# A third column pair computed by seven products, with the keys' rotation beside them, in a Trainium2 encoder block

## The chip, the cores and the metric

The kernel runs on one core of a Trainium2 chip. The metric is device time in microseconds (us) of one whole execution, the median of three. Engines are named as in the profile: PE (TensorE, matrix products) with PEld (its weight loads), DVE (VectorE), ACT (ScalarE), POOL (GpSimd) and SP (SyncE, which here only issues transfers). Each engine executes its own list of instructions in order; an instruction that waits for another engine or for a transfer (a DMA) holds back all that stand behind it in the same list.

## What is computed

One layer of an encoder, for two requests (512 and 256 positions, 768 rows in all, width 2048), with shared weights. Cut to what matters here:

```python
h = rmsnorm(x, ln_mix_g);  z = h @ w_in            # 2560 columns
zf = z[..., :1024]   # 8 Fourier groups of 128 channels
q  = z[..., 1024:2048] # 16 query heads of 64
k, v = z[..., 2048:2304], z[..., 2304:]   # 4 heads each
of = per group: Re(fft2(zf)) @ w_fourier[g]
q, k = apply_rope(q), apply_rope(k)      # x*cos + rot(x)*sin
s = q @ k.T * 64**-0.5, within +-128 positions
m = maximum(max(s), sink);  p = exp(s - m) / (sum exp(s - m) + exp(sink - m))
x = x + concat(rmsnorm(of), rmsnorm(p @ v)) @ w_out
x = x + relu(rmsnorm(x) @ w_up)**2 @ w_down;  return rmsnorm(x)
```

All of it is in 32-bit floats. The kernel splits each operand into a high and a low part (`wh`, `wl` for weights) and sums three products of parts, so one product of the reference is three matmuls. ACT makes a high part (a copy that rounds), DVE the low part (a subtraction).

## The kernel before

The columns of `w_in` are worked in blocks of 256. First come the values `v`. Then 8 Fourier blocks of 128 channels, that is two pairs of 256-column blocks, are computed by **seven products**: a 2x2 block scheme with seven block products (`a11`, `s1`, `s2`, `s3`, `a22`, `s4`, `a12`) in place of eight. A step is one half of one product for one column block pair: 28 steps (`NP7`), each with 24 matmuls of 128x384 (`product7`, L277). In step n the code adds the weights of step n+3 where the scheme wants a sum (`sum7`, DVE), makes their high part (`high7`, ACT) and the low part of step n+2 (`low7`, DVE), and takes the results of step n-1 out of PSUM (`out7`): a copy on ACT (L297) or an add on DVE (L294), then a store of `z` to DRAM. The order on SP, ACT and DVE in this stage is the order of the code ("manual schedule").

The rest of the columns (keys, 2048 on, and four query blocks) come as 20 **pieces** of 48 matmuls of 128x384 (L830), four pieces for one pair of column halves. The weights of piece p+2 are split while piece p runs (`piece_split`, L69 for `wh`, L70 for `wl`). Among the pieces the 8 Fourier groups are done, one per piece: `fold`, `stage1` (three blocks, whose results become `ah` on ACT and `al` on DVE) and `stage2` (18 matmuls of 128x256, L659), whose result `of` POOL squares and sums (L669, L670) and ACT stores to DRAM (`ofd`). After the eighth group come the rotations: POOL multiplies with the sines (`cross`, L715), DVE with the cosines and adds (`turned`, L722 and L724), ACT and DVE split the result (`parts`, L740 and L741) and ACT stores it. A table `after(piece, fn)` says in which half piece each of these is written; outside the last piece a scheduler in the compiler may place it differently. In the last piece the order on SP, ACT, DVE and POOL is the code's own again. Finally `load_of(0)` loads the first Fourier results back (`ofr`), which the output projection (`pm`, L1077) splits (`ofh` on ACT, `ofl` on DVE) and multiplies between the attention products (L876 `s`).

In attention, DVE adds the mask and takes the maximum of each row in one instruction (L891), a second instruction negates it (L896), and ACT applies the exponential (L906).

Of the kernel before, what the change touches and what calls it, by code (L numbers as in the profile page):

```python
# [40 lines left out]
def hybrid_encoder(ctx: ExitStack, tc: tile.TileContext, a: dict):  # L41
# [75 lines left out]
    kr_d = dpool.tile([4 * P, T], F32, tag="k", name="k")  # L117
    qr_d = [[dpool.tile([2 * P, T], F32, tag=f"q{c}{i}", name=f"q{c}{i}") for c in "hl"] for i in range(NKV)]
# [79 lines left out]
    with ExitStack() as ph:  # L198
        hp = ph.enter_context(tc.tile_pool(name="hp", bufs=1, reuse_waits="tile"))
        pp = ph.enter_context(tc.tile_pool(name="pp1", bufs=4, space=PSUM))  # L200
# [7 lines left out]
        NP7 = 4 * len(names7)  # L208
# [5 lines left out]
        def load7(n):  # L214
            if n >= NP7:
                return
            x, g, e = names7[n // 4], n // 2 % 2, n % 2
            blocks = blocks7.get(x, (x,))
            raw7[n] = []
            for i, x in enumerate(blocks):  # L220
# [6 lines left out]
                nc.sync.dma_start(raw[:], w_in[2 * g + c][:, k0 : k0 + 4, :])  # L227
                raw7[n].append(raw)

        def sum7(n):  # L230
            if n >= NP7:
                return
            s, ge = names7[n // 4], n % 4
            x = raw7[n][0]
            if s == "s1":
                kept7[ge] = hq["p"].tile([P, 4, 256], F32, tag="ws", name="ws", bufs=4)
# [28 lines left out]
        def product7(n):  # L265
            w, g, e = n // 4, n // 2 % 2, n % 2
            bank = bank7[names7[w]]
            opens = w == 0 or names7[w] in ("s1", "a12")
            wh, wl = w7.pop(n)
            if e == 0 and opens:  # L270
                for r in range(2):
                    ps7[bank, g, r] = pp.tile([P, 512], F32, **(dict(tag="f", bufs=4) if bank == "Y" and 2 * g + r < 4 else dict(tag="ps", bufs=4)), name="p7")
            x = xs[w % 2]
            for i in range(4):
                for r in range(2):
                    for q, (l, o) in enumerate(((wh, 0), (wh, 1), (wl, 0))):
                        nc.tensor.matmul(  # L277
                            ps7[bank, g, r][:, :HALF], l[:, i, r * P : (r + 1) * P], x[:, o, 4 * e + i, :],
# [4 lines left out]
        def out7(n):  # L283
            while put7:
                put7.pop(0)()
            if n < 0 or n % 2 == 0:
                return
            s, g = names7[n // 4], n // 2 % 2
            c, t, how = take7[s]
            for r in range(2):  # L290
                ps = ps7[bank7[s], g, r][:, :HALF]
                if how == 1:
                    z = c7.pop((c, t, g, r))
                    nc.vector.tensor_tensor(out=z[:], in0=ps, in1=z[:], op=ALU.add)  # L294
                else:
                    z = hq["p"].tile([P, HALF], F32, tag=f"z{c}{t}", name="z7", bufs=2 if how else 4)
                    nc.scalar.activation(z[:], ps, AF.Copy)  # L297
                if how == 0:
                    c7[c, t, g, r] = z
                else:  # L300
                    dst = zf_d[4 * g + 2 * c + r]
# [1555 lines left out]
```

## Time and profile before

| | |
|---|---|
| median of three executions | 2574.53 us (2574.41 to 2574.83) |
| profiled execution, its own time | 2575.42 us |
| span of its trace | 2573.6 us |
| PE busy | 2561.6 us, 100% of the span |
| DVE / ACT / POOL busy | 70% / 44% / 10% |
| granted TensorE clock | 0.999 of full speed |
| seven products | 42.16 to 158.60 us |
| pieces | 158.60 to 362.39 us |
| attention with half of the output projection | from 362.39 us |

A busy share is the time in which an engine executes; an idle engine matters only if another waits for it. The chain of waits goes back from the last instruction to what released each one, so it names the engine that set the time. The windows table gives the same busy times for a stretch. The time of a group of instructions is the mean of one instruction; in a dense row of matmuls their distance is what counts, since a matmul's own time overlaps with the next one's.

### The profile page before, as it was taken

How to read it: one execution, taken by the hardware profiler on the slowest of the kernel's cores; microseconds unless marked ns; L12 is line 12 of the kernel's file. 1: busy time of each engine (PE TensorE's matmuls, PEld its weight loads, DVE VectorE, ACT ScalarE, POOL GpSimd, SP SyncE). 2: the span in 40 equal slices, each digit the busy share in tenths (PEclk: the TensorE clock that was granted, in tenths of full speed). 3: DMA queues.
4: the chain of work that ended last, by engine and by line, in shares of the span. 5: the costliest groups of instructions: out<-in, count | busy, mean ns of one | idle time of the engine just before them, and what ended most of it. 6: DMA issues, size and time to landing. Idle time of an engine off the chain costs nothing.

```text
span 2573.6 us, 34809 instructions
## 1 busy us (share of the span) xinstructions
PE 2561.6 (100%) x13467; PEld 2345.1 (91%) x13467; DVE 1797.7 (70%) x2222; ACT 1122.4 (44%) x1621; POOL 246.3 (10%) x345
## 2 busy tenths in 40 slices
PE   9999999999999999999999999999999999999998
PEld 9999998888899999999999999988888888888887
DVE  8866467786565565556777777667766766777687
ACT  7645337683234333333445544433333333333335
POOL 0102322223201001100000000100000000000000
PEclk9999999999999999999999999999999999999999
DMA  8753567455655455456666666775543662555364
GB/s 303 230 184 126 168 194 209 137 163 190 227 180 176 153 174 173 164 184 239 218 230 230 214 217 211 262 290 176 176 155 118 217 229 84 175 185 159 101 210 152
DMA packets 259815, 487.84 MB, mean 190 GB/s; under 512 B 20602, under 2 KB 147328, under 8 KB 259392
## 3 DMA queue, kind: packets, MB, share of 16 engines
q1 hardware_dynamic: 188112, 321.77, 39.1%
q10 hardware_dynamic: 58512, 112.05, 11.5%
q0 software_dynamic: 13024, 51.79, 6.0%
q8 instruction: 106, 1.74, 0.3%
q14 instruction: 61, 0.50, 0.1%
HBM read 365.99 MB, written 119.54 MB: 189 GB/s over the span
## 4 chain that ended last, share of the span: by engine, by line
PE 97%; DVE 2%; DMA 1%; ACT 0%; issue 0%; SPq 0%; DVEq 0%; POOLq 0%; POOL 0%; ACTq 0%
PE pu L1224 36%; PE pd L1659 35%; PE pm L1077 9%; PE pz L830 6%; PE p L277 5%; PE pv L442 1%; PE o L955 1%; PE t L933 1%; PE s L876 1%; PE pe L659 0%; PE pa L638 0%; PE ptx L137 0%; DVE p L891 0%; DMA ofr<-ofd 0%; DVE ofl L1061 0%
## 5 line engine op out<-in xcount | busy, mean ns | idle before, releaser
L1224 PE MATMUL pu<-xf,wh 128*128 128x384 f32 x3072 | 780.2, 334 | 0.0
L1224 PEld LDWEIGHTS pu<-xf,wh 128*128 128x128 f32 x3072 | 554.1, 188 | 1.5 <-ACT o L1242 1.2
L1659 PE MATMUL pd<-wl,sh 128*128 128x512 f32 x1332 | 517.7, 389 | 0.0
L1659 PE MATMUL pd<-wh,sh 128*128 128x512 f32 x1332 | 517.7, 389 | 0.0
L1659 PE MATMUL pd<-wh,sl 128*128 128x512 f32 x1332 | 517.5, 389 | 0.0
L1224 PE MATMUL pu<-xf,wl 128*128 128x384 f32 x1536 | 513.2, 334 | 0.0
L1636 ACT ACTIVATE wh<-rd 128x1024 fp32r<-128x1024 f32 x200 | 202.4, 1054 | 522.2 <-PE pd L1659 414.2
L1646 DVE TENSOR_TENSOR wl<-rd,wh 128x1024 fp32r<-128x1024 f32 x200 | 236.1, 1221 | 226.3 <-ACT wh L1636 225.5
L1204 ACT ACTIVATE wh<-ur 128x1024 fp32r<-128x1024 f32 x160 | 170.1, 1063 | 382.5 <-PE pu L1224 208.0
L1659 PEld LDWEIGHTS pd<-wh,sh 128*128 128x128 f32 x1332 | 250.1, 188 | 51.8
L1659 PEld LDWEIGHTS pd<-wh,sl 128*128 128x128 f32 x1332 | 250.0, 188 | 51.9 <-DVE sl L1647 0.3
L1659 PEld LDWEIGHTS pd<-wl,sh 128*128 128x128 f32 x1332 | 250.1, 188 | 51.6
L1224 PEld LDWEIGHTS pu<-xf,wl 128*128 128x128 f32 x1536 | 288.3, 188 | 0.0
L1210 DVE TENSOR_TENSOR wl<-ur,wh 128x1024 fp32r<-128x1024 f32 x160 | 195.4, 1221 | 76.1 <-ACT wh L1204 76.1
L1245 DVE TENSOR_TENSOR o<-pu,o 128x768 f32<-128x768 f32 x160 | 152.8, 956 | 122.3 <-PE pu L1224 114.8
L1629 DVE TENSOR_TENSOR rd<-rd 128x1024 f32<-128x1024 f32 x112 | 131.7, 1217 | 0.0
L1224 PE MATMUL pu<-xs,wh 128*128 128x384 f32 x512 | 129.8, 334 | 0.0
L1204 ACT ACTIVATE wh<-sx 128x1024 fp32r<-128x1024 f32 x64 | 67.9, 1062 | 130.6 <-PE pu L1224 101.9
L277 PE MATMUL p<-xs,wh 128*128 128x384 f32 x448 | 113.9, 334 | 0.0
L1647 DVE TENSOR_TENSOR sl<-sr,sh 128x768 fp32r<-128x768 f32 x111 | 105.5, 951 | 0.0
L1210 DVE TENSOR_TENSOR wl<-sx,wh 128x1024 fp32r<-128x1024 f32 x64 | 78.2, 1222 | 23.8 <-ACT wh L1204 23.6
L1224 PEld LDWEIGHTS pu<-xs,wh 128*128 128x128 f32 x512 | 92.4, 188 | 0.0
(293 smaller groups left out, 3849.3 us busy)
## 6 DMA issues: line engine op xcount, KB each, us to landing
rd<-in_w_down SPq DMA_DIRECT2D x176, 512.0 KB, 5.2
ur<-in_w_up SPq DMA_DIRECT2D x128, 512.0 KB, 3.9
sr<-sd SPq DMA_DIRECT2D x95, 384.0 KB, 5.4
pd<-o ACTq DMA_DIRECT2D x60, 384.0 KB, 2.3
o<-pd POOLq DMA_DIRECT2D x60, 384.0 KB, 6.1
sd<-sm ACTq DMA_DIRECT2D x60, 384.0 KB, 2.7
raw<-in_w_in SPq DMA_DIRECT2D x39, 512.0 KB, 4.3
raw<-in_w_out SPq DMA_DIRECT2D x32, 512.0 KB, 4.5
```

The source lines that it names most:

```text
L277: nc.tensor.matmul(ps7[bank, g, r][:, :HALF], l[:, i, r * P : (r + 1) * P], x[:, o, 4 * e + i, :], start=(opens and e == 0 and i == 0 and ...
L830: nc.tensor.matmul(ps[c][s][:, :HALF], w[:, i, cs], whole[j // 2][s][o][:, 4 * (j % 2) + i, :], start=first and n == 0, stop=stop and n == 2,)
L1077: nc.tensor.matmul(ps, l(k), w[:, k % 2, :], start=(k == 0 and n == 0), stop=(k == 7 and n == 2))
L1204: nc.scalar.activation(wh[:], raw[:], AF.Copy)
L1210: nc.vector.tensor_tensor(out=wl[:], in0=raw[:], in1=f32(wh[:]), op=ALU.subtract)
L1224: nc.tensor.matmul(ps[:, t, :HALF], w[:, i, t * P : (t + 1) * P], xb[:, o, i, :], start=(s == first_of[bank] and i == 0 and n == 0), stop= ...
L1245: nc.vector.tensor_tensor(out=o, in0=src, in1=o, op=ALU.add)
L1629: add = lambda x, y, op: nc.vector.tensor_tensor(out=x[:], in0=x[:], in1=y[:], op=op)
L1636: nc.scalar.activation(wh[:], t[:], AF.Copy)
L1646: nc.vector.tensor_tensor(out=wl[:], in0=t[:], in1=f32(wh[:]), op=ALU.subtract)
L1647: nc.vector.tensor_tensor(out=sl[:], in0=sr[:], in1=f32(sh[:]), op=ALU.subtract)
L1659: nc.tensor.matmul(o, l[:, q, ts], w[:, ns], start=(j == j0 and (q, t) == (0, 0)), stop=(j == j1 and (q, t) == (1, 2)),)
```

## The change

A third pair of column blocks, the keys (block 8) and one quarter of the queries (block 6), joins the seven products: 42 steps instead of 28, and 12 pieces instead of 20. `a11`, `s2`, `s3` and `a22` accumulate in six PSUM banks; `s1`, `s4` and `a12` share two further banks, which the next group of columns reuses. In each step the result of the step before is taken out first, and the first half of a step's own result right behind its product. The product's loop over its two row halves is the outer one. The keys are rotated in steps 29 to 40, in buffers of that stage; the cosines and sines, multiplied with the norm factor, go to DRAM and come back for the queries. The Fourier groups are written half a piece or more earlier, the other rotations among them. In attention mask, sink and queries are negated, and a minimum takes the place of maximum and negation.

```diff
-        NP7 = 4 * len(names7)
+        cols7 = ((0, 1), (2, 3), (6, 8))
+        NS7 = 2 * len(cols7)
+        NP7 = NS7 * len(names7)
...
         def product7(n):
...
-            for i in range(4):
-                for r in range(2):
+            for r in range(2):
+                if e == 0 and opens:
+                    ps7[own, g, r] = pp.tile([P, 512], F32, tag="t" if own else "x", bufs=2 if own else 6, name="p7")
+                for i in range(4):
...
+        def k_tables():
+            for name, src in (("cos", a["c_cos"]), ("sin", a["c_sin"])):
+                kr[name] = spare7()[:].rearrange("p a b -> p (a b)")[:, :T]
+                nc.sync.dma_start(kr[name], src)
...
+        def k_scale():
+            for name in ("cos", "sin"):
+                nc.vector.tensor_tensor(out=kr[name], in0=kr[name], in1=rb[:], op=ALU.mult)
...
+            for s in range(3):
+                step(k_at, 33 + 2 * s, lambda s=s: k_cross(s))
+                step(k_at, 34 + 2 * s, lambda s=s: k_turn(s))
+                step(k_at, 35 + 2 * s, lambda s=s: k_parts(s, 35 + 2 * s))
+            step(k_at, 29, k_tables)
+            step(k_at, 32, k_loads)
+            step(k_at, 32, k_scale)
+            step(k_at, 33, k_keep)
             for n in range(NP7):
-                for fn in high_at.get(n, ()):
-                    fn()
+                out7(n - 1, 1)
                 sum7(n + 3)
                 high7(n + 3)
                 low7(n + 2)
+                product7(n)
+                out7(n, 0)
...
-                product7(n)
-                out7(n - 1)
...
-            out7(NP7 - 1)
-            out7(-1)
+            out7(NP7 - 1, 1)
+            stores7()
+        pctx.close()
...
-        for pair, t, ahead in ((0, 10.5, 10), (2, 11.5, None), (3, 15, None), (1, 16.5, 12)):
...
+        for pair, ts in ((1, (2, 4, 6)), (2, (7.5, 8, 8.5)), (3, (9, 9.5, 10))):
+            for s, t in enumerate(ts):
+                after(t, lambda pair=pair, s=s: cross(pair, s))
+                after(t + 0.5, lambda pair=pair, s=s: (turned(pair, s), parts(pair, s)))
...
-        after(18, lambda: load_of(0, [kt["kp"].tile([P, 4, P], F32, tag="zy", name="ofr", bufs=2) for _ in range(2)]))
-        n_in = 4 * len(cols)
+        after(10.5, lambda: load_of(0, [kt["kp"].tile([P, 4, P], F32, tag="zy", name="ofr", bufs=2) for _ in range(2)]))
+        n_in = 4 * (len(cols) - 2)
...
-                scalar=sink[:, 4 * g + h : 4 * g + h + 1], op0=ALU.add, op1=ALU.max, accum_out=mx[:, h : h + 1],
+                scalar=sink[:, 16 + 4 * g + h : 17 + 4 * g + h], op0=ALU.add, op1=ALU.min, accum_out=nm[:, h : h + 1],
...
-        nc.vector.tensor_scalar(out=st["nm"][:, hs], in0=mx[:, hs], scalar1=-1.0, scalar2=None, op0=ALU.mult)
```

Three places show what that does to the lists. The first is the seam from the seven products to the pieces, on ACT. `z7` is a result of the seven products on its way to DRAM, `wh` the high part of a piece's weights, `tabh` that of a Fourier table. Before:

```order
L69 ACTIVATE wh_1841<-raw_1836 128x1024
L302 DMA zf4_74<-z7_1264 128x384
L302 DMA zf5_75<-z7_1266 128x384
L72 ACTIVATE xf01_1613<-d7_1685,gall_256 128x384 x4
L69 ACTIVATE wh_1847<-raw_1838 128x1024
L302 DMA zf0_70<-z7_898 128x384
L302 DMA zf1_71<-z7_900 128x384
L69 ACTIVATE wh_1857<-raw_1845 128x1024
```

In the change:

```order
L327 DMA zs1_79<-z7_2146 128x384
L327 DMA zs1_79<-z7_2148 128x384
L69 ACTIVATE tabh_2373<-tab_2381 128x512
L69 ACTIVATE tabh_2373<-tab_2382 128x512
L69 ACTIVATE wh_2405<-raw_2385 128x1024
L69 ACTIVATE wh_2411<-raw_2389 128x1024
```

Before, `wh_1841`, the weights of piece 0, stands ahead of six of the last stores; in the change `wh_2405`, the weights of piece 0, stands behind the last store (`z7_2148`, the second half of step 41) and behind two table splits.

The second is DVE among the pieces. `zs_2805` is a query pair under rotation, `zy_3748` POOL's product for its last third, `of_2989` the result of Fourier group 2, and `al_2885` the low part that `stage2` of group 3 multiplies. In the change:

```order
L340 TENSOR_TENSOR zs_2805<-zs_2805,cosr_2394 128x2x256
L352 SCALAR_TENSOR_TENSOR zs_2805<-zs_2805,zh_3674 128x2x256
L782 TENSOR_SCALAR of_2989<-pz2_2970 128x256
L342 TENSOR_TENSOR zs_2805<-zs_2805,zy_3679 128x256 x2
L750 TENSOR_TENSOR ft_3002<-pa_2997,ft_3002 128x256
L352 SCALAR_TENSOR_TENSOR zs_2805<-zs_2805,zh_3743 128x2x256
L340 TENSOR_TENSOR zs_2805<-zs_2805,cosr_2394 128x2x256
L70 TENSOR_TENSOR al_2885<-ft_3002,ah_2884 128x256
L342 TENSOR_TENSOR zs_2805<-zs_2805,zy_3748 128x256
L709 TENSOR_TENSOR zf_3084<-zf_3084,rb_286 128x768
L70 TENSOR_TENSOR al_2885<-pa_3007,ah_2884 128x256
```

and on POOL, at the same place:

```order
L336 TENSOR_TENSOR zy_3679<-zs_2805,sinr_2396 128x256 x2
L787 TENSOR_TENSOR sq_2992<-of_2989 128x768
L788 TENSOR_TENSOR ssf_2375<-ssf_2375,sq_2992 128x768
L336 TENSOR_TENSOR zy_3748<-zs_2805,sinr_2396 128x256 x2
```

Before, no rotation stood among the `al` rows of a Fourier group; in the change the second L340 row, which waits for `zy_3748`, stands ahead of all of group 3's `al` rows, and `zy_3748` stands on POOL behind the squares of group 2.

The third is the start of attention, on DVE. `wl_3877` and `wl_3928` are low parts that follow the last piece's first half, `ofl0` is the low part of the first Fourier results. Before:

```order
L70 TENSOR_TENSOR wl_3844<-raw_3690,wh_3843 128x1024
L70 TENSOR_TENSOR wl_3877<-raw_3769,wh_3876 128x1024
L843 COPY zs_3873<-pz_3603 128x384
L843 COPY zs_3873<-pz_3604 128x384
L1061 TENSOR_TENSOR ofl0_3926<-ofr_3837,ofh0_3925 128x512
L1061 TENSOR_TENSOR ofl0_3926<-ofr_3838,ofh0_3925 128x512
```

In the change:

```order
L70 TENSOR_TENSOR wl_3928<-raw_3810,wh_3927 128x1024
L340 TENSOR_TENSOR zs_3424<-zs_3424,cosr_2394 128x2x256
L342 TENSOR_TENSOR zs_3424<-zs_3424,zy_3884 128x256 x2
L352 SCALAR_TENSOR_TENSOR zs_3424<-zs_3424,zh_3934 128x2x256
L939 COPY zs_3924<-pz_3552 128x384
L939 COPY zs_3924<-pz_3553 128x384
L1153 TENSOR_TENSOR ofl0_3988<-ofr_3944,ofh0_3987 128x512
L1153 TENSOR_TENSOR ofl0_3988<-ofr_3945,ofh0_3987 128x512
```

The last third of the next-to-last rotation (`zs_3424`) now stands behind `wl_3928`, and the buffer of its `zy_3884` is the one that `ofr_3944` takes (tag `zy`, two buffers). PE's list is the same at this place before and after: the last pieces' matmuls, one pair of `s`, then `pm` with `ofh0`.

## Rows read from the trace of the kernel before

**Rows 1.** The page's first part: busy us of each engine, share of span.

```profile
PE 2561.6 (100%) x13467; PEld 2345.1 (91%) x13467; DVE 1797.7 (70%) x2222; ACT 1122.4 (44%) x1621; POOL 246.3 (10%) x345
```

**Rows 2.** Windows table: length, then busy PE, PEld, DVE, ACT, POOL; clock, DMA.

```profile
42.00:100.00 58.00, 58.00 (x337) 58.00 (x336) 52.22 (x41) 36.40 (x48) 3.42 (x6) 1.00 0.63 210
...
158.00:260.00 102.00, 102.00 (x669) 102.00 (x668) 62.40 (x144) 46.41 (x124) 17.20 (x11) 1.00 0.44 139
```

**Rows 3.** PE's waits from 158 to 700 us: total, times, longest.

```profile
PE s L876 <- DVE mx L891: 0.8, 1, 0.8
```

**Rows 4.** DVE groups, 40 to 160 us: busy, mean ns, idle before.

```profile
L262 DVE TENSOR_TENSOR wl<-raw,wh 128x1024 fp32r<-128x1024 f32 x7 | 8.5, 1215 | 0.0
L308 DVE TENSOR_TENSOR xr<-xr,xr 128x1536 f32<-128x1536 f32 x5 | 8.7, 1747 | 0.0
L294 DVE TENSOR_TENSOR z<-p,z 128x384 f32<-128x384 f32 x11 | 5.6, 549 | 0.0
L73 DVE SCALAR_TENSOR_TENSOR xf<-d,gall,xf 128x384 fp32r<-128x384 f32 x8 | 4.4, 614 | 7.9 <-ACT xf L72 7.9
```

**Rows 5.** ACT's list at the seam: two issues of stores (start, us).

```profile
156.19 0.92 ACTq L302 DMA_DIRECT2D zf<-z  x2
```

**Rows 6.** ACT groups, 158 to 420 us.

```profile
L69 ACT ACTIVATE wh<-raw 128x1024 fp32r<-128x1024 f32 x26 | 27.5, 1056 | 26.3 <-PE pz L830 17.8 <-DMA raw<-in_w_in 4.1 <-DVE zs L741 2.7
...
L69 ACT ACTIVATE tabh<-tab 128x512 fp32r<-128x512 f32 x2 | 1.3, 634 | 4.7 <-DMA tab<-in_c_pos 4.7
...
L1060 ACT ACTIVATE ofh<-ofr 128x512 fp32r<-128x512 f32 x2 | 1.2, 632 | 0.0
```

**Rows 7.** DVE groups, 158 to 420 us.

```profile
L724 DVE TENSOR_TENSOR zs<-zs,zy 128x256 f32<-128x256 f32 x28 | 13.3, 510 | 0.1
L722 DVE TENSOR_TENSOR zs<-zs,cosr 128x512 f32<-128x512 f32 x14 | 12.2, 873 | 8.7 <-POOL zy L715 8.7
L741 DVE SCALAR_TENSOR_TENSOR zs<-zs,zh 128x512 fp32r<-128x512 f32 x11 | 8.4, 783 | 1.7 <-ACT zh L740 1.7
...
L591 DVE TENSOR_TENSOR zf<-zf,rb 128x768 f32<-128x768 f32 x8 | 7.6, 951 | 7.4 <-DMA zf<-zf 7.4
...
L896 DVE TENSOR_SCALAR nm<-mx 128x1 f32<-128x1 f32 x27 | 4.1, 154 | 0.9
...
L664 DVE TENSOR_SCALAR of<-pz 128x256 f32<-128x256 f32 x8 | 3.4, 422 | 18.6 <-PE pz L659 18.6
```

**Rows 8.** POOL groups, 158 to 420 us.

```profile
L715 POOL TENSOR_TENSOR zy<-zs,sinr 128x256 f32<-128x256 f32 x28 | 27.0, 991 | 51.6 <-ACT zs L843 21.5 <-DVE ofl L1061 18.2 <-DVE zs L724 9.9
L670 POOL TENSOR_TENSOR ssf<-ssf,sq 128x768 f32<-128x768 f32 x7 | 13.0, 1851 | 0.5
L669 POOL TENSOR_TENSOR sq<-of 128x768 f32<-128x768 f32 x7 | 10.3, 1468 | 67.2 <-DVE of L664 56.0 <-DMA zf<-zf 11.2
```

**Rows 9.** PE's list: last of one group's stage 2, first of the next one's.

```profile
205.32 0.28 PE L659 MATMUL pz<-tabh,al 128*128 128x256 f32 x1
...
216.10 0.28 PE L659 MATMUL pe<-tabh,ah 128*128 128x256 f32 x1
```

**Rows 10.** DVE's list between them: first and last of the next group's `al`.

```profile
208.98 0.91 DVE L70 TENSOR_TENSOR al<-ft,ah 128x256 fp32r<-128x256 f32 x1 [2.09 <-ACT ah L69]
...
215.17 0.28 DVE L70 TENSOR_TENSOR al<-pa,ah 1x128 fp32r<-1x128 f32 x1
```

**Rows 11.** ACT's list at the start of attention.

```profile
358.25 0.86 ACT L843 COPY zs<-pz 128x384 f32<-128x384 f32 x2 [4.61 <-PE pz L830]
359.00 1.07 ACT L69 ACTIVATE wh<-raw 128x1024 fp32r<-128x1024 f32 x1
```

**Rows 12.** DVE's list there.

```profile
360.10 1.23 DVE L70 TENSOR_TENSOR wl<-raw,wh 128x1024 fp32r<-128x1024 f32 x1 [5.21 <-ACT wh L69]
```

**Rows 13.** PE's list there: the first `pm` behind the pieces.

```profile
362.62 0.40 PE L1077 MATMUL pm<-wh,ofh 128*128 128x512 f32 x1
```

**Rows 14.** DMA issues, 335 to 365 us: count, KB each, us to landing.

```profile
ofr<-ofd SPq DMA_DIRECT2D x2, 256.0 KB, 4.1
```

More of the change, by code (lines that the diff above doesn't have):

```diff
@@ L216, in load7 @@
                 return
[L217 removed]
+            x, g, e = of7(n)
             blocks = blocks7.get(x, (x,))
@@ new lines, in back7, with cross_of, turned_of @@
+        def back7(g):
+            for r in range(2):
+                z = c7[2, g, r] = tile7("z11", NS7)
+                nc.sync.dma_start(z[:], home7(g, 0, r)[:, :HALF])
+        def cross_of(z, y, sin):
+            for b in range(2):
+                nc.gpsimd.tensor_tensor(out=y[:, b], in0=z[:, 1 - b], in1=sin, op=ALU.mult)
+        def turned_of(z, y, cos):
+            cb = cos.rearrange("p (o t) -> p o t", o=1).to_broadcast([P, 2, 256])
+            nc.vector.tensor_tensor(out=z, in0=z, in1=cb, op=ALU.mult)
+            for b, op in enumerate((ALU.subtract, ALU.add)):
+                nc.vector.tensor_tensor(out=z[:, b], in0=z[:, b], in1=y[:, b], op=op)
@@ new lines, in parts_of @@
+        def parts_of(z, hi, out, scale, s, when=lambda dt, fn: fn(), dts=(0, 0)):
+            ts = slice(s * 256, (s + 1) * 256)
+            put = lambda o, x: nc.scalar.dma_start(out[o][:, ts].rearrange("(b p) t -> p b t", p=P), x)
+            if scale is None:
+                nc.scalar.activation(hi, z, AF.Copy)
+                low = lambda: nc.vector.tensor_tensor(out=z.bitcast(F32R), in0=z, in1=f32(hi), op=ALU.subtract)
+            else:
+                nc.scalar.activation(hi, z, AF.Copy, scale=scale)
+                low = lambda: nc.vector.scalar_tensor_tensor(
+                    out=z.bitcast(F32R), in0=z, scalar=scale, in1=f32(hi), op0=ALU.mult, op1=ALU.subtract
+                )
+            when(0, lambda: put(0, f32(hi)))
+            when(dts[0], low)
+            when(dts[1], lambda: put(1, z))
@@ L304, in part, with k_parts, stores7 @@
+        def k_parts(s, n):
+            parts_of(kr["z"][s], kr["hi"][:, s % 2], k_out, None, s, lambda dt, fn: step(k_at, n + dt, fn), (1, 2))
+        k_at = {}
+        def stores7(left=0):
+            while len(put7) > left:
+                put7.pop(0)()
         def part(x, e):
@@ L434, in prepare @@
                         split(*parts[t], raw[t])
-            pv = [pp.tile([P, 512], F32, tag="f" if m < 4 else "ps", bufs=4, name="pv") for m in range(NM)]
+            pv = [pp.tile([P, 512], F32, tag="x", bufs=6, name="pv") for m in range(NM)]
             def v_term(c, m, term, i):
@@ L534, in hybrid_encoder @@
         ):
+            for tag, shape, bufs in (("z10", [P, HALF], 2), ("d7", [P, 4, HALF], 1), ("z01", [P, HALF], NS7)):
+                hq["p"].tile(shape, F32, tag=tag, name="z7", bufs=bufs)
             for n in range(2, 5):
@@ L543, in hybrid_encoder @@
                 low7(n + 2)
+                product7(n)
+                out7(n, 0)
+                for fn in high_at.get(n, ()):
+                    fn()
                 for fn in low_at.get(n, ()):
                     fn()
-                product7(n)
-                out7(n - 1)
+                for fn in k_at.get(n, ()):
+                    fn()
+                stores7(1 if n % 2 else 0)
                 load7(n + 5)
```

283 lines of the change are left out of this document (148 added, 135 removed).

## The prediction

> **What bounds the kernel now.** I read the busy times first. PE is busy in 2561.6 of the span's 2573.6 us [rows 1], so the time is PE's list plus the few moments at which PE has nothing ready. The windows say where: through the seven products and through the pieces PE is busy in every microsecond, 58.00 of 58.00 and 102.00 of 102.00, at clock 1.00 [rows 2]. PE's waits from the pieces to the end of the projection hold a single row, 0.8 us behind DVE's row maximum [rows 3]. The reader is to see two things: fewer matmuls pay in full, and there is no idle time that could swallow a new wait, so every microsecond for which PE's next operand is late is added to the time.
>
> **What is removed.** 14 more steps of 24 matmuls are 336, 8 fewer pieces of 48 are 384: 48 matmuls of 128x384 less. In the seven products 337 matmuls take 58.00 us [rows 2], 0.172 us each, so 48 save **8.3 us**. Everything else on PE stays. DVE loses 96 negations of 154 ns [rows 7], 14.8 us of DVE time, but PE waits for that chain for 0.8 us only [rows 3]; I take 0.5 us, between 0 and 0.8. The splits of 8 pieces go from the pieces and those of 14 steps are added before; they lie beside matmuls.
>
> The rest is a search for operands that come late. I follow the lists in the five places where the order shows new work ahead of something that PE needs.
>
> **Step 34.** `s4` of the third pair needs a PSUM bank which step 33's first half leaves, by an add on DVE. From the add of step 31's first half, half a step (2.1 us) into that step, DVE's list holds, up to and with that of step 33: three adds at 0.549, one input difference at 1.747, three splits or sums at 1.215 (a sum has the split's shape, two inputs of 128x1024), four L73 at 0.614 [rows 4], two table multiplications at 0.951 (nearest shape) [rows 7]. With one more split that is 1.65 + 1.75 + 4.86 + 2.46 + 1.90 = 12.6 us, behind 2.1: 14.7 against 3 steps of 24 x 0.172 = 12.4. DVE's neighbours overlap a little at their ends (eight L73 of 614 ns were busy for 4.4 us only) [rows 4], so the lower bound is 0 and the upper 2.3; I take **0.6**, since the sum is just full.
>
> **The seam.** In the change, the high part of piece 0's weights stands on ACT behind the store of the very last seven-product result and two table splits. That store waits for DVE's add, which waits for PE's last matmul. So PE ends, then: add 0.549 [rows 4], issue of the store 0.46 (two in 0.92) [rows 5], two `tabh` at 0.634 and `wh` at 1.056 [rows 6]: 3.3 us. The low part, 1.215 [rows 4], begins behind `wh`, and only four matmuls of 0.172 can run before it: 0.5 more. **3.9 us** with a semaphore or two. Nothing covers it, because PE's list has nothing but piece 0 there. Bounds 3.0 (if table splits overlap with the add) and 5.
>
> **stage2 of group 0.** Ahead of the last `al` rows DVE has a fold's multiplication 0.951, two L342 (as L724, 0.510) and an L352 (as L741, 0.783) that did not stand there: 2.75 us [rows 7]. Before, the last `al` was done at 215.45 and PE began the stage at 216.10 [rows 9, 10]: 0.65 us to spare. So up to 2.1; I take **1.2**, bounds 0 and 2.3.
>
> **stage2 of group 3.** Here DVE waits for POOL with all of the group's `al` rows behind. After a group's last stage-2 matmul at 205.5 [rows 9] DVE began the next `al` at 208.98 [rows 10], 3.5 us later. In the change that row stands behind an L340 which waits for `zy_3748`, and POOL reaches that behind the squares of group 2: taking `of` 0.422 [rows 7], 1.468 + 1.851 + 2 x 0.991 = 5.3 [rows 8], L340 0.873: 6.6 us after the stage. That is 3.1 later, two L342 before the group's last `al` make it 4.1, less 0.65 to spare: 3.5. `of_2989` itself stands behind another L340 that waits for POOL's products, and an L352: up to 2 us more. I take **4.3**, bounds 0 (if the rotation runs so early that POOL is through before) and 5.5. Before, the same wait of L722 for POOL is there, 8.7 us in all [rows 7], but nothing that PE needed stood behind it.
>
> **Start of attention.** Before, the last piece's first half was taken out from 358.25 and `pm` began at 362.62 without a wait [rows 11, 13]. In the change `ofr_3944` can be loaded only when the last third of a rotation has left its buffer, and that third stands on DVE behind `wl_3928`, behind `wh_3927` on ACT, behind the copies of the last piece's first half. From the first copy: `wh` begins 0.75 later and takes 1.07 [rows 11], `wl` 1.23 [rows 12], L340 0.873, two L342 1.02 [rows 7], transfer 4.1 [rows 14], `ofh` 0.632 [rows 6]: 9.7 us, against the 4.4 after which PE stands at `pm`. A quieter DMA could land sooner, by 1 us at most, I estimate. That is 4.3 to 5.3. The second half, `ofr_3945`, comes later still (its buffer waits for a store), with PE working some 3 us on the first: 0 to 2. I take **5.5** in all, bounds 4 and 7.5.
>
> **The sum.** Against the profiled execution of 2575.4 us: -8.3 - 0.5 + 0.6 + 3.9 + 1.2 + 4.3 + 5.5 = +6.7, thus 2582.1; the median of the runs shown stands 0.9 lower, so **2581.2, told as 2581 us**. The change takes 48 matmuls away and puts some 15 us of waits in.
>
> **The clock.** The clock is 1.00 where PE is never idle [rows 2]; no row of before has PE idle for as long as the start of attention would have it. The Trainium skill (TensorE: Matmul & The Clock Gate, section "HAM oscillation — how this bites in real kernels") says that PE's clock falls to half after an idle gap; by that rule the sum would be larger, and no run here shows it. As a mechanism of this kernel: if the matmuls after the 5 us stop ran at the lower level, 1.2 GHz, for as long as the stop was, those 5 us would yield 2.5 us of work, so +2.5, and as much again at the seam: up to 2586.
>
> **The rivals.**
> - *The full gain, faster.* The waits named are in lists of engines with 30% and more to spare [rows 1], and if their work runs ahead at the seam, at group 3 and at `ofr`, PE keeps what 48 matmuls give: 2574.5 - 8.3 - 0.5 = 2565.7. It is one mechanism, slack: it decides once the seam, group 3 and attention together cost under about 3.6 us. Against it: at the seam and at attention the chain begins with PE's own last matmul, so no engine can run ahead of it. Chance 0.17, times to 2569.3.
> - *Only PE's own chains count, no difference.* POOL is through early, stage 2 costs nothing and `ofr` lands in 3 us: -8.8 + 0.6 + 3.9 + 4 = -0.3, 2574; all of the group 0 wait still fits. Chance 0.23, from 2569.4 to 2579.7.
> - *Starved steps, slower still.* In the seven products DVE is busy for 52.22 of 58.00 us [rows 2], and the change adds more adds, a rotation and loads there. If each of the 14 added steps falls behind by what DVE is short, say 0.3 us at step 34's rate (0.6 for two steps), that is 4 more: 2585; with twice that 2590. For it: the list is full at step 34. Against: in the first half as full a list made no wait. Chance 0.13.
> - *The clock*, as above, 2584 to 2586: chance 0.07.
> - The forecast, 2580 to 2584: chance 0.40.
>
> **How the numbers follow.** 0.2% is 5.1 us, about what a measurement of this kernel can tell from no change: 2569.4 to 2579.7. Faster 0.17, same 0.23, slower 0.40 + 0.13 + 0.07 = 0.60. The sum's own bounds are -8.3 - 0.8 + 0 + 3 + 0 + 0 + 4 = -2.1 to -8.3 + 2.3 + 5 + 2.3 + 5.5 + 7.5 = +14.3, that is 2572 to 2589. The range takes in part of the other cases: 2569 to 2591, which leaves out some 0.17 below and little above.
>
> **What would show it.** In the profile of the changed kernel, PE's waits between 200 and 400 us should be named: `pz` behind ACT's `wh` at about 217 us for 3 to 4 us, `pe` or `pz` of one Fourier group behind `al` or `ah` near 283 for some 4, `pm` behind `ofh` near 364 for 4 to 5, and a wait of under 1 us near 181. The seven products should end near 217, 42 + 42 x 4.15. The prediction is wrong if PE has no wait at the seam, if `ofr` is issued well before the last piece's middle, or if the seven products themselves stretch.

## The result: slower by 12 us, and the profile after

The changed kernel takes 2586.9 us (median of four, 2585.8 to 2591.9) against 2574.5 us (2574.4 to 2574.8): ratio 1.0049, 95% interval 1.0037 to 1.0062. The profiled execution of after is one of 2586.7 us, its span 2584.9. Since executions of the changed kernel scatter by some 6 us, with a mean granted clock from 0.997 to 0.995, a difference of 2 us between two versions of it is read from their lists below and not from their times alone. The first part of its page, to be read beside [rows 1] (busy us, share of span, instructions):

```profile
PE 2561.3 (99%) x13419; PEld 2342.9 (91%) x13419; DVE 1810.4 (70%) x2153; ACT 1124.5 (44%) x1621; POOL 249.2 (10%) x345
```

48 matmuls are gone, as the diff says, and yet PE was busy for as long as before, where 8.3 us less were to be expected. Some 4.7 us of this are matmuls that ran at half clock (below). The rest was not followed in full; a part lies right behind the waits, where a matmul of 256 columns shows 0.38 us instead of 0.28. The waits of PE from 40 to 700 us say where it stood still; before, the part from the pieces on held one row of 0.8 [rows 3] (total us, times, longest):

```profile
PE pm L1169 <- ACT ofh L1152: 3.8, 1, 3.8
PE pz L930 <- ACT wh L69: 3.2, 1, 3.2
PE pz L777 <- DVE al L70: 2.2, 3, 1.0
PE p L287 <- DVE z L301: 1.4, 1, 1.4
PE pc L713 <- ACT of L779: 1.3, 2, 0.8
PE s L970 <- DVE es L990: 0.6, 1, 0.6
```

The windows table of the same profile shows what a list of waits doesn't: three stretches at half clock (columns as in [rows 2]; the clock is the number behind POOL's).

```profile
217.00:225.00 8.00, 4.52 (x24) 3.89 (x23) 4.71 (x7) 2.98 (x4) 0.00 (x0) 0.98 0.56 185
225.00:228.00 3.00, 3.00 (x11) 3.00 (x11) 2.89 (x9) 0.83 (x7) 0.00 (x0) 0.50 0.90 329
...
296.00:300.00 4.00, 3.54 (x13) 3.54 (x14) 1.11 (x2) 2.52 (x6) 3.30 (x2) 0.57 0.62 202
...
375.00:378.00 3.00, 3.00 (x9) 2.41 (x9) 0.18 (x1) 0.84 (x2) 1.43 (x2) 0.50 0.83 240
```

From 225 to 228 us PE counts as busy in every microsecond and still does 11 matmuls where it does 17 at 173 ns: the clock stands at its lower level, 1.2 GHz. Each such stretch lies behind a wait. In this execution it begins 2.1 us after PE has gone on at the seam (222.7, 224.8) and 0.7 us after it at attention (374.3, 374.9), and at group 3 just as `pc` ends its wait (296.4, 296.5). A busy share can't tell such a stretch from full work; the clock and the count of matmuls can.

For an account in one unit I take each matmul's time from its start to the next one's, less the median of its shape (173 ns for 384 columns, 120 for 256, 111 for 128), and sum what is over, by place. From the first matmul of the seven products to the first `pm` behind the pieces, before lost 1.1 us in this way.

| place (us in after) | forecast | lost in after |
|---|---|---|
| 48 matmuls less | -8.3 | -8.3 |
| seven products but step 34 (42 to 217) | 0 | 1.4 |
| step 34 (184) | 0.6 | 1.6 |
| seam (219 to 224.6) | 3.9 | 4.0 |
| half clock behind it (to 228) | 0 | 1.6 |
| group 0 (250 to 252) | 1.2 | 1.9 |
| `pc` at 279 | 0 | 0.7 |
| group 3 (290 to 294) | 4.3 | 2.7 |
| `pc` at 295, half clock to 300 | 0 | 1.0 + 1.7 |
| start of attention (370 to 374) | 5.5 | 4.0 |

That is 20.6 - 1.1 - 8.3 = +11.2 of the 11.8 us by which the first `pm` comes later, counted from the first product (332.46 against 320.63 us); the other 0.6 us are spread over the stretch in small amounts. Behind the first `pm` nothing is lost or won: from there to the first matmul of the up projection it is 354.0 us against 354.2, half clock and all. By the same account before lost 3.6 us in the first 65 us of that stretch, and after 3.4, of these 1.4 at half clock.

### The profile page after: what moved, and what is told of

The parts are those of the page before. It is cut to its first block, busy times and chain, and to the rows that moved or that the text cites. A ratio compares the mean times of both kernels' runs of the same rounds, so it can differ in the third digit from the quotient of the medians.

```text
span 2584.9 us, 34679 instructions
## 1 busy us (share of the span) xinstructions
PE 2561.3 (99%) x13419; PEld 2342.9 (91%) x13419; DVE 1810.4 (70%) x2153; ACT 1124.5 (44%) x1621; POOL 249.2 (10%) x345
## 4 chain that ended last, share of the span: by engine, by line
PE 91%; DVE 3%; DMA 2%; issue 1%; ACT 1%; POOL 1%; SPq 0%; ACTq 0%; POOLq 0%; DVEq 0%
PE pu L1316 36%; PE pd L1751 35%; PE pm L1169 9%; PE p L287 3%; PE pz L930 2%; PE pv L538 1%; PE o L1047 1%; PE s L970 1%; PE t L1025 1%; DMA raw<-in_w_in 1%; PE ptx L138 0%; DMA zf<-z 0%; DVE wl L70 0%; POOL zy L336 0%; DMA z<-zf 0%
## 5 line engine op out<-in xcount | busy, mean ns | idle before, releaser
L287 PE MATMUL p<-xs,wh 128*128 128x384 f32 x672 | 170.8, 335 | 1.9 <-DVE z L301 1.4
L287 PEld LDWEIGHTS p<-xs,wh 128*128 128x128 f32 x672 | 121.0, 188 | 2.9 <-issue 1.7
L287 PE MATMUL p<-xs,wl 128*128 128x384 f32 x336 | 112.3, 334 | 0.0
```

The costliest lines, as they stand in the source:

```text
L287: nc.tensor.matmul(ps7[own, g, r][:, :HALF], l[:, i, r * P : (r + 1) * P], x[:, o, 4 * e + i, :], start=(opens and e == 0 and i == 0 and q ...
```

## The three large waits, read in the lists

**The seam.** ACT's list in after (start, us; behind the bracket what ended its idle time), then PE's:

```profile
218.04 2.45 ACTq L327 DMA_DIRECT2D zs<-z  x2
220.54 1.15 ACT L69 ACTIVATE tabh<-tab 128x512 fp32r<-128x512 f32 x2 [13.89 <-DMA zs<-z]
221.59 1.04 ACT L69 ACTIVATE wh<-raw 128x1024 fp32r<-128x1024 f32 x1
```

```profile
219.16 0.34 PE L287 MATMUL p<-xs,wl 128*128 128x384 f32 x1
222.68 0.97 PE L930 MATMUL pz<-xf,wh 128*128 128x384 f32 x4 [3.19 <-ACT wh L69]
223.94 0.61 PE L930 MATMUL pz<-xf,wl 128*128 128x384 f32 x2 [0.29 <-DVE wl L70]
```

The second store waits for the add behind PE's last product, and both table splits and `wh` stand behind it: the chain of the forecast, link by link, 3.2 us and then 0.3 for `wl`.

**Group 3.** DVE's list, then POOL's:

```profile
280.94 0.41 DVE L782 TENSOR_SCALAR of<-pz 128x256 f32<-128x256 f32 x1
...
286.88 0.69 DVE L340 TENSOR_TENSOR zs<-zs,cosr 128x512 f32<-128x512 f32 x1 [1.33 <-POOL zy L336]
287.49 0.42 DVE L70 TENSOR_TENSOR al<-ft,ah 128x256 fp32r<-128x256 f32 x1
...
293.83 0.27 DVE L70 TENSOR_TENSOR al<-pa,ah 1x128 fp32r<-1x128 f32 x1
```

```profile
281.50 1.51 POOL L787 TENSOR_TENSOR sq<-of 128x768 f32<-128x768 f32 x1 [1.80 <-DVE of L782]
283.09 1.91 POOL L788 TENSOR_TENSOR ssf<-ssf,sq 128x768 f32<-128x768 f32 x1
284.96 1.89 POOL L336 TENSOR_TENSOR zy<-zs,sinr 128x256 f32<-128x256 f32 x2
```

`al` stands on DVE behind L340, that behind POOL's `zy`, that behind the squares of group 2, which wait for `of` from DVE. The last `al` row, at 293.83, is read by the last matmul of the stage. That matmul in after, and then the one before the change that reads the `al` of 215.17 in [rows 10]:

```profile
294.15 0.39 PE L777 MATMUL pz<-tabh,al 128*128 128x256 f32 x1
```

```profile
218.13 0.28 PE L659 MATMUL pz<-tabh,al 128*128 128x256 f32 x1
```

Before, the last `al` was done 2.7 us (215.45 to 218.13) ahead of the matmul that reads it; in after nothing is left of that.

**The start of attention.** ACT's list and SP's:

```profile
370.44 0.63 ACT L351 ACTIVATE zh<-zs 128x512 fp32r<-128x512 f32 x1 [2.69 <-DVE zs L342]
371.10 0.37 ACTq L346 DMA_DIRECT2D qh<-zh  x1
371.83 0.37 ACTq L346 DMA_DIRECT2D ql<-zs  x1
373.58 0.63 ACT L1152 ACTIVATE ofh<-ofr 128x512 fp32r<-128x512 f32 x1 [2.51 <-DMA ofr<-ofd]
```

```profile
370.44 6.74 SPq L189 DMA_DIRECT2D ofr<-ofd  x5
```

SP issues `ofr` in the very moment in which `zh` has its input, and `ofh` follows 3.1 us later. Before, `pm` began there without a wait [rows 13].

## Experiments

All of them are runs of changed versions of after, but for x5, which is a version of before. The kernel before, run beside them, had medians from 2574.4 to 2574.8.

**Pieces 0 and 1 prepared early (x1).** Their weights are loaded and split in the last steps of the seven products.

```diff
+                if n >= NP7 - 2:
+                    early["w", n - NP7 + 2] = wsplit(early.pop(n - NP7 + 2))
+                if n in (NP7 - 5, NP7 - 4):
+                    j = n - NP7 + 5
+                    early[j] = wload(w_in[4][:, 4 * j : 4 * j + 4, :], 4, 256)
-        piece_split(0)
-        piece_split(1)
+        in_w[0], in_w[1] = early.pop(("w", 0)), early.pop(("w", 1))
```

> The changed kernel with one edit: the weights of pieces 0 and 1 are loaded and split inside the last steps of the seven products, ahead of the last stores and of the table splits, instead of behind them. Theory (the seam's wait is ACT's list: add, store, two table splits, wh): the 3.4 us wait of pz behind wh and the 0.5 behind wl go, and with them the stretch at half clock that follows (11 matmuls at 320 instead of 173 ns, 1.7 us): 2586.9 - 5.6 = about 2581. If the clock's fall has nothing to do with the wait, 1.7 us stay: 2583. Rival (the wait only moves, because tables or Fourier group 0 come later by as much): 2584 to 2587, with a new wait of stage 1 or 2 of group 0.

Measured: 2581.1 (2579.6 to 2585.2), ratio 1.0024 [1.0015, 1.0034]. The seam's wait is gone and the clock behind it stays up, as the window shows that stood at 0.50 in after, and group 0 has no wait either; a wait of 1.3 for `wf` and one of 1.5 for `qs`, both on DMAs, came in. So the 5.9 us are a net of more than the seam: 4.0 there, 1.6 of half clock and 1.9 at group 0 went, and some of it came back elsewhere.

```profile
225.00:228.00 3.00, 3.00 (x19) 3.00 (x18) 2.87 (x6) 1.21 (x7) 0.00 (x0) 1.00 0.92 319
```

**Pair 3 turned half a piece earlier (x2).**

```diff
-        for pair, ts in (... (3, (9, 9.5, 10))):
+        for pair, ts in (... (3, (8.5, 9, 9.5))):
```

> The changed kernel with one edit: the three thirds of the next-to-last rotation stand half a piece earlier (8.5, 9, 9.5 for 9, 9.5, 10), so the buffer that the first Fourier results are loaded into is free before the last piece. Theory (pm waits because that buffer is freed by work behind the last piece's own splits): the 4.0 us wait of pm behind ofh goes and the half-clock stretch behind it (1.8 us): 2586.9 - 5.8 = about 2581. Rival (the rotation then stands among the last Fourier group's al rows and costs there what it cost at group 3): 2.5 to 4 us come back, 2584 to 2585.

Measured: 2582.5 (2579.8 to 2585.7), ratio 1.0031 [1.0021, 1.0042], 1.5 us above the first theory. `pm` no longer waits and the clock there stays up; in exchange some 2.7 us are lost between 310 and 360 us, where a group's stage 2 now stands behind the earlier rotation.

**The sine products of pair 2 on VectorE (x3).**

```diff
-                nc.gpsimd.tensor_tensor(out=y[:, b], in0=z[:, 1 - b], in1=sin, op=ALU.mult)
+                eng.tensor_tensor(out=y[:, b], in0=z[:, 1 - b], in1=sin, op=ALU.mult)
```

> The changed kernel with one edit: the sine products of the first query pair rotated among the pieces (pair 2 of the table) run on DVE instead of POOL; DVE gets six more products of 128x256 of about 0.42 us. Theory (stage 2 of Fourier group 3 is late because DVE's list stands at a row that waits for POOL): the 2.7 us of waits there, the 1.0 us of pc behind it and the half-clock stretch (1.7 us) go: 2586.9 - 5.4 = about 2581.5. Rival (DVE has simply too much work there): no gain, 2587 to 2589.

Measured: 2585.0 (2580.6 to 2587.7), ratio 1.0039 [1.0027, 1.0050]. The gain of 2.0 us is not clear of the scatter (the interval overlaps with that of after), and the profiled execution is the shortest of the six, 2580.6, near the 2581.5 of the first theory. In its lists the waits of group 3's stage 2 are gone and no half clock follows, so POOL was what held group 3. Why the median lies 4.4 us above this execution, no trace shows. `pc` waits longer here, since `of` now stands behind the rotation on ACT:

```profile
PE pc L713 <- ACT of L779: 1.9, 1, 1.9
```

**Fillers at the seam and at attention (x4).** 25 and 33 small matmuls whose result nobody reads, put into PE's list where it waits.

```diff
+            pw = pp.tile([P, 512], F32, tag="f", bufs=4, name="pw")
+            for _ in range(n):
+                nc.tensor.matmul(pw[:, :P], ones[:], ones[:], start=True, stop=True)
```

> The changed kernel with one addition: 25 matmuls of 128x128 on constants, into a free PSUM bank, stand on PE at the seam, and 33 at the start of attention; they fill some 2.7 and 3.6 us of the two long waits and change no operand's time. Theory (TensorE's clock falls because PE stood idle): granted clock 1.00 behind both places, the stretches at 320 and 427 ns per matmul are gone, the waits themselves end when they did: 2586.9 - 3.5 = 2583.4; the stretch behind group 3 stays. Rival (the matmuls are slow there for another reason, such as the transfers that run at the same time): the same stretches at the same places, 2586.9 or more.

Measured: 2589.4 (2587.4 to 2591.3), ratio 1.0057 [1.0042, 1.0072]. Each call shows as two rows of 111 ns pitch, so the fillers took 5.5 and 7.3 us and overran the waits by 2.2 and 3.6. The clock stayed at 1.00 in both places. So the time says nothing on the cost of the clock; x7 and x10 to x12 use fewer fillers.

**The minimum alone (x5)**, in the kernel before:

```diff
-                scalar=sink[:, 4 * g + h : 4 * g + h + 1], op0=ALU.add, op1=ALU.max, accum_out=mx[:, h : h + 1],
+                scalar=sink[:, 16 + 4 * g + h : 17 + 4 * g + h], op0=ALU.add, op1=ALU.min, accum_out=nm[:, h : h + 1],
```

> The kernel before with one part of the change alone: the minimum of negated scores in place of the maximum, so that the negation of each maximum (DVE, four per group and pass) falls away and exp takes scale -1. The forecast's term for this is -0.5 us, between 0 and -0.8, so 2574.2 against 2574.7: a difference that five rounds can hardly tell from none. If the s <- DVE mx waits of before (0.8 us in all) stay as s <- DVE nm waits of the same size, the term was nothing; if this part alone made the kernel slower by 2 us or more, it would belong into the 5 us that the sum of the forecast lacks.

Measured: 2574.2 (2573.2 to 2575.0) beside 2574.6, ratio 0.9997 [0.9988, 1.0006]: the sign fits, the size can't be told from nothing. In its profile the one row of [rows 3] is gone, and PE has no wait from 158 to 700 us. This part cost no time.

**The split of the input's first rows two steps later (x6).**

```diff
-            step(low_at, 32 + 4 * e, lambda e=e: first_split(e))
+            step(low_at, 34 + 3 * e, lambda e=e: first_split(e))
-                step(low_at, 32, lambda: first_load(1))
+                step(low_at, 34, lambda: first_load(1))
```

> The changed kernel with the second weights of the pieces (first_load(1), and the split that it feeds) moved two steps later, from steps 32 and 36 to steps 34 and 37 of the seven products. Theory: the 1.4 us wait of p behind DVE z at 184.2 us comes from the split that stands in the same step on DVE as the result that PE waits for; it goes, so 2586.9 - 1.6 = 2585.3, and no clock is gained or lost, because no half-clock stretch followed that wait. Rival: DVE is full all through steps 30 to 37 (no idle time from 172 to 186 us), so the wait only moves two steps on and the time is 2586.9; or the split then comes too late for the first groups, and pz waits at the seam for 1 to 2 us more.

Measured: 2585.0 (2582.6 to 2587.7), ratio 1.0040 [1.0027, 1.0054]; no wait is left at 184 us. The 1.9 us are not clear of the scatter either, so the lists have to show the cause. What the edit moves is not weights, as the expectation has it, and not the L273 row, but the split of the input's first rows (`xf`, four L73 rows on DVE). DVE's list in after, where PE waits for the first of the two adds (L301):

```profile
180.28 2.21 DVE L73 SCALAR_TENSOR_TENSOR xf<-d,gall,xf 128x384 fp32r<-128x384 f32 x4 [0.56 <-ACT xf L72]
182.40 1.82 DVE L379 TENSOR_TENSOR kr<-kr,rb 128x768 f32<-128x768 f32 x2
184.15 1.22 DVE L273 TENSOR_TENSOR wl<-raw,wh 128x1024 fp32r<-128x1024 f32 x1
185.28 1.01 DVE L301 TENSOR_TENSOR z<-p,z 128x384 f32<-128x384 f32 x2
```

In x6 the L73 rows stand behind the adds, and the first add begins at 183.03:

```profile
183.03 0.55 DVE L301 TENSOR_TENSOR z<-p,z 128x384 f32<-128x384 f32 x1
...
186.82 2.19 DVE L73 SCALAR_TENSOR_TENSOR xf<-d,gall,xf 128x384 fp32r<-128x384 f32 x4
```

**Fillers of half the number (x7)**, 12 and 16:

> The changed kernel with filler matmuls before the pieces and before the first pm of attention again, but half as many: 12 and 16 calls, which at 2 x 109 ns each (measured in the run with 25 and 33) are 2.6 and 3.5 us, shorter than the waits of about 3.3 and 3.9 us there. Theory (the half-clock stretches come from the waits and cost 1.6 and 1.8 us): both stretches go, nothing is overrun, and the time is 2586.9 - 3.4 = 2583.5. Rival: the idle time that is left (about 0.7 and 0.4 us at each place, before or behind the fillers) is enough for the clock to fall, or the small matmuls do not keep it up at this count: then the stretches stay and the time is 2586.9.

Measured: 2588.6 (2587.3 to 2591.0), ratio 1.0055 [1.0041, 1.0069]: a miss. The clock is 1.00 behind both places and nothing is overrun. But in the profiled execution, the longest of the four (2591.0), the wait at step 34 was 1.8 us long (1.4 in after) and the clock fell behind that one, and again at group 0 and group 3; group 0 lost 3.2 us instead of 1.9. Behind step 34:

```profile
187.50:190.50 3.00, 3.00 (x11) 3.00 (x11) 2.97 (x4) 0.00 (x0) 3.00 (x3) 0.50 0.95 359
```

**Everything that took a wait away, together (x8)**: the edits of x1, x2 and x6, the sine products of pairs 2 and 3 on VectorE, and

```diff
             load_weight(0)
+            load_weight(1)
             tabs = [...]
```

This last line loads `wf`, the Fourier weights of the second group, for which PE waited in x1; the expectation calls it the columns.

> The changed kernel with everything of which a run or the trace says that it takes a wait away, together: pieces 0 and 1 loaded and split inside the seven products (-5.9 in its own run), pair 3 turned a half piece earlier (-4.5), the sine products of pairs 2 and 3 on VectorE instead of GpSimd (-2, and it should take away the waits that the earlier turn brought at 345 us), the second weights two steps later (-1.5), the columns of the second group loaded before the pieces. Theory: the change's gain is there, 8.3 us of matmuls, and what is lost of it is lost only to these waits and to the clock behind them. Then the sum is 2586.9 - 5.9 - 4.5 - 2 - 1.5 = 2573.0 at least, and with the waits of x1 and x2 that were new (about 3 and 2.7 us) also gone 2567 to 2570, faster than before by 5 to 8 us. Rival: VectorE, now with the split and the sine products as well, ends late in the pieces (its al and wl behind pz), each wait that is gone comes back as another one, and the time is 2576 to 2582.

Measured: 2571.4 (2570.4 to 2575.1), ratio 0.9990 [0.9982, 0.9999], faster than before by 3.2 us. The single runs x1, x2, x3 and x6 gained 5.9, 4.5, 2.0 and 1.9 against after (the last two not clear of the scatter); their sum leads to 2572.7. The seam, group 3's stage 2, step 34 and `pm` have no wait any more. Two rows are left, and some 1.1 us of half clock behind the first of them (2571.4 - 1.9 - 1.8 - 1.1 would be 2566.6). So the time lies above the 2567 to 2570 of the first theory by what moved on to `pc` and by a weight load that came late in the products (at 74 us DVE stands idle for 1.7 us until it has landed):

```profile
PE pc L720 <- ACT of L786: 1.9, 1, 1.9
PE p L287 <- ACT z L308: 1.8, 1, 1.8
```

**`ofr` in buffers of its own (x9).**

```diff
-        ... kt["kp"].tile([P, 4, P], F32, tag="zy", name="ofr", bufs=2) ...
+        ... kt["kq"].tile([P, 4, P], F32, tag="ofr", name="ofr", bufs=2) ...
```

> The changed kernel, with the two ofr tiles of the first attention blocks in buffers of their own instead of those of zy. In the changed kernel ofr's loads are issued at 370.4 us, at the moment when ACT's zh has read the last zy, and pm starts 3.95 us late at 374.3. First theory (the step of the prediction: the buffer holds the load): the loads are issued some 6 us earlier, right behind the last qs load, the wait of pm goes entirely and with it the half-clock stretch behind it, 2586.9 - 3.9 - 1.4 = 2581.6. Second theory (ACT's queue holds it as well): the load is early, but ofh stands on ACT behind zh, which starts at 370.44 here, and behind the issues of two stores; so ofh starts at about 372.2 instead of 373.6, the wait of pm shrinks only to about 2.6, the clock falls behind it all the same, and the time is 2585.6.

Measured: 2585.5 (2585.2 to 2589.8), ratio 1.0042 [1.0029, 1.0056]. The 1.4 us are not clear of the scatter, and the profiled execution is the longest of the four, so its lists count here and its time doesn't. SP issues `ofr` 5.9 us ahead of `zh`, and `ofh` is late all the same, behind `zh` and two issues:

```profile
376.07 0.63 ACT L351 ACTIVATE zh<-zs 128x512 fp32r<-128x512 f32 x1 [2.69 <-DVE zs L342]
376.73 0.37 ACTq L346 DMA_DIRECT2D qh<-zh  x1
377.46 0.37 ACTq L346 DMA_DIRECT2D ql<-zs  x1
377.87 1.15 ACT L1152 ACTIVATE ofh<-ofr 128x512 fp32r<-128x512 f32 x2 [1.17 <-DVE zs L352]
```

```profile
PE pm L1169 <- ACT ofh L1152: 2.5, 1, 2.5
```

So the wait has two causes in a row: the buffer is worth 1.3 us, and what is left is ACT's order, which x2 dealt with by letting the rotation end earlier.

**Fillers again, without the wait at step 34 (x10)**: x6 and the 12 and 16 fillers.

> The changed kernel with the second weights two steps later, as in the run that took away the wait at 184 us (2585.0), and with the 12 and 16 short fillers at the seam and at the start of attention. In that run PE lost 1.0 us to half clock at 223 to 225 us and 1.4 us at 372.6 to 375.2, and the waits ahead of them are 3.3 and 3.8 us, longer than the fillers' 2.8 and 3.5. Theory: the half-clock stretches of these two places go, nothing else changes, 2585.0 - 2.4 = 2582.6. Rival (what the first run with short fillers showed: the stretches went from the filled places, but the clock was low at 187, 258 and 302 us instead, 2.5 us in all): a half-clock stretch comes behind other waits, at group 0 or group 3, and the time stays at 2585.

Measured: 2589.9 (2588.1 to 2591.5), ratio 1.0055 [1.0042, 1.0069]: a miss by 7 us, with the clock up behind both places. Then each filler alone, at the seam (x11) and at attention (x12):

> The changed kernel with the second weights two steps later (2585.0 in its own run) and the 12 short fillers at the seam alone. Both fillers together gave 2589.9 where 2582.6 was expected. First theory: the half clock behind the seam (1.0 us) is not on the path, because group 0's stage 2 ends at a time that the load of pair 1's columns sets: in five profiles its last wait ends 20.6 to 21.4 us behind GpSimd's first zy, whatever PE did before, so time that the filler saves comes back as a longer wait for al (0.7 us without, some 1.7 with it), and the time stays at 2585.0. Second theory: this filler itself costs the 4.9 us, for instance since its PSUM buffer shifts those of the Fourier groups behind it: then 2589 here.

> The same with the 16 short fillers at the start of attention alone. First theory: half clock at 372.6 to 375.2 us costs 1.4 us, but in the run with both fillers 0.9 us of it came back as waits for the next ofh, so 2585.0 - 0.5 = 2584.5. Second theory: the loss of 4.9 us comes from this filler: 2589 to 2590. If both single fillers give 2585, the loss comes from the two together or from a part of the program that is neither, and stays open.

Measured: 2585.7 (2585.1 to 2587.0), ratio 1.0043 [1.0026, 1.0060], and 2584.8 (2584.1 to 2586.0), ratio 1.0041 [1.0026, 1.0056]. Both rule out the 2589 of the second theories: neither filler alone costs or gains anything that can be measured. A gain of 1 us, though, these times couldn't tell from none; that there is none at the seam is read at group 0. POOL's first `zy` (it waits for the load of pair 1's columns), and PE's last wait in that group, in x11:

```profile
230.03 1.79 POOL L336 TENSOR_TENSOR zy<-zs,sinr 128x256 f32<-128x256 f32 x2 [36.30 <-DMA zs<-zs]
```

```profile
251.05 0.39 PE L777 MATMUL pz<-tabh,al 128*128 128x256 f32 x1 [0.54 <-DVE al L70]
```

The distance is 21.0 us here, with the clock up. In after it is 20.7, with half clock:

```profile
231.68 1.43 POOL L336 TENSOR_TENSOR zy<-zs,sinr 128x256 f32<-128x256 f32 x2 [39.32 <-DMA zs<-zs]
```

```profile
252.35 0.38 PE L777 MATMUL pz<-tabh,al 128*128 128x256 f32 x1 [0.54 <-DVE al L70]
```

In x6, x7, x9 and x10 it is 20.6 to 21.4 as well. So in this order of DVE's list group 0 ends when DVE and POOL have turned pair 1, whatever PE did. (x1 and x8 have another order there, with the first `al` rows ahead of the rotation: 15.8 and 12.2 us, and no wait.) In x12 the clock fell while PE still waited at the seam, PE then ran at half clock for 5.8 us, and there is no wait at group 0 at all:

```profile
218.60:220.60 2.00, 0.00 (x0) 0.00 (x0) 0.93 (x2) 1.04 (x2) 0.00 (x0) 1.00 0.63 239
220.70:221.70 1.00, 0.00 (x0) 0.00 (x0) 0.83 (x3) 0.96 (x2) 0.00 (x0) 0.50 0.46 66
221.71:227.48 5.77, 5.77 (x18) 5.65 (x19) 4.76 (x9) 1.51 (x6) 0.00 (x0) 0.50 0.97 338
```

What this does to the time, from the starts of three rows in each run (the last matmul of the seven products, POOL's first `zy`, the last matmul of group 0's stage 2; us):

| run | half clock behind the seam | last product to first `zy` | `zy` to group 0's last matmul | together | lost at group 0 |
|---|---|---|---|---|---|
| after | 3.4 | 12.5 | 20.7 | 33.2 | 1.9 |
| x6 | 3.4 | 10.5 | 21.4 | 31.9 | 0.9 |
| x11 | none | 10.9 | 21.0 | 31.9 | 2.2 |
| x12 | 5.8 | 10.2 | 21.6 | 31.8 | 0 |

With the same edit at step 34, x6, x11 and x12 take the same time from the last product to the end of group 0, at either level of the clock. At attention the filler of x12 took the half clock away, and PE then waited 1.0 us for the second `ofh`, which in x6, at half clock, it reaches without a wait:

```profile
375.64 0.50 PE L1175 MATMUL pm<-wh,ofh 128*128 128x512 f32 x1 [0.99 <-ACT ofh L1158]
```

Another 0.4 within `pm` and 0.9 ahead of `s` are left behind it in x12. What stays open: why both fillers together took 4 us more than either alone. The profile of x10 has 1.5 us of half clock at 13 us, in a part that no edit touches, and starts its products 2.4 us late, but that is one execution of five.

## Why the prediction held, and where its sum was short

The direction and the kind of cause were right: the gain of 48 matmuls is there, and operands that come late cost more. x8 shows it from the other side: with most of the waits taken out, the same matmuls make the kernel faster. All five places named have the wait, behind the engine named. The number was less good: 2586.9 lies above the forecast's own 2580 to 2584, and it is the width of the range, 2569 to 2591, that holds it. One of the signs of being wrong came true in small: the seven products did stretch, to 177.4 us where 42 x 4.15 are 174.3. By steps:

- *-8.3 for the matmuls*: nothing contradicts it; in x8, late starts from the first product to the first `pm` are 7.5 us against 1.1 before, and 7.5 - 1.1 - 8.3 = -1.9 is just what was measured for that stretch.
- *The negations, -0.5*: 0.4 measured, not distinguishable from nothing.
- *Step 34, 0.6*: 1.6, inside its bounds; of 0 to 2.3, 0.6 was too kind. The four L73 rows of the sum, 2.2 us, are what the list is over by: x6 puts them behind the awaited add, and the wait is gone.
- *The seam, 3.9*: 4.0 lost.
- *Group 0, 1.2*: 1.9. The rows counted are there, but what starts them is the load of pair 1, whose landing varies, and PE's own pace decides the rest: the loss ranges from none (x12) to 3.5 us (x9).
- *Group 3, 4.3*: 2.7, and 1.0 at `pc` behind it, which had no term. The place and the cause (POOL behind the squares) stand, by x3. That the size lies within its bounds is in part luck, since two of its parts were wrong in opposite directions. The chain is later than counted: `al` begins 9.4 us behind group 2's last stage-2 matmul (278.05 to 287.49), 5.8 more than before (205.32 to 208.98), where 3.1 and up to 2 were expected: `of` was taken 2.9 us behind that matmul (280.94), where before it was 0.3 (205.64). And the time to spare was not 0.65 us: that ends at the first matmul of the stage, but the last `al` is read by its last one, 2.7 us after it was done. So 5.8 - 2.7 = 3.1, about what the account has with 2.7 in the stage and 0.7 at the `pc` ahead of it (279).
- *Attention, 5.5*: 4.0. The wait for the first half lies below the 4.3 to 5.3 that were worked out, since the load landed in 3.1 us and not in 4.1. A wait for the second half doesn't show in after, where PE ran at half clock meanwhile; at full clock it does, with 1.0 us in x12. And the buffer, named as the cause, is the first of two (x9).
- *The clock*: the largest of the terms that the sum had at nothing. It was put among the rivals with 0.07, and it did happen, behind the seam, group 3 and the stop at attention, with 1.6, 1.7 and 1.4 us; the rival's 2.5 each is too high. The Trainium skill (TensorE: Matmul & The Clock Gate, section "HAM oscillation — how this bites in real kernels") says that the clock falls after an idle gap; the trace agrees, 0.50 behind a wait of 3.2 us. The same section of the Trainium skill prices a throttled stretch at half its length; here x6, x11 and x12 show that this is no sure loss, since the wait behind it can take it up. So the 1.6 us behind the seam are booked to the clock, but with the clock up most of them would have come back as a longer wait at group 0.

The sum in one line: to the forecast's +6.7 come step 34 with 1.0, the seam 0.1, group 0 0.7, the negations that gave nothing 0.5, and what had no term: the other products 1.4, the two `pc` 1.7, half clock 3.3, less the 1.1 that before lost too. Group 3 and attention give back 1.6 and 1.5. That is +11.2, and +11.3 is what the two profiled executions differ by.

Of the rivals, *the full gain* fell by x1: the chain at the seam begins with PE's own last product, and only work done ahead of it takes it away. *Only PE's own chains count* fell by groups 0 and 3. *Starved steps* has its 1.4 us, not 4, and the largest wait of theirs in any trace, step 34 aside (1.8 us, x8), comes from a load that landed late and not from a full list.

## What to carry to other kernels

Where PE is busy all the time, removing matmuls pays only as much as the lists of the other engines allow: go through them at each place where the first operand of a stage depends on the last result of the one before, and move its preparation ahead of that result (5.9 us in x1) before counting the gain. Count the time to spare up to the instruction that reads the last operand, not up to the start of its stage. A wait has often a second cause right behind the first, a queue behind a buffer, so take out one and look again. Price a slow stretch by what comes next: if the next wait is set by another engine, as at group 0 here, running faster before it gains nothing.

## What the hardware showed unexpectedly

- PE's clock fell to half at different moments of the same wait: at the seam, where PE stood for 3.2 us in after and 3.1 in x12, it fell 2.1 us after PE had gone on in after (224.8 us), and while PE still stood in x12 (between 220.6 and 220.7 us). PE then worked at half clock for 3.4 us in after and for 5.8 in x12.
- The length of the last wait alone didn't decide: behind 1.8 and 1.9 us at step 34 the clock fell (x7, x9), behind 1.4 at the same place in after it didn't; behind 1.9 us at `pc` it stayed at 1.00 in x3 (292.9 to 296 us), and in x8 it was at 0.50 (261.4 to 264.4).
- One call of a 128x128 matmul on operands typed fp32 gave two rows, 111 ns apart (116 rows for 58 calls in x4); calls on operands typed fp32r give one.
- In no profile of before or of x5 did the clock fall between 42 and 700 us; in every profile with the third column pair in the seven products it fell at least once.
